# One FFN half-step with the activations as TensorE's stationary operand and 512 weight columns as its moving one

## The chip, the cores and the metric

The kernel runs on one core of a Trainium2 chip. TensorE (PE) multiplies a stationary 128x128 operand, which a weight load (PEld) brings in ahead, with a moving operand of up to 512 columns, into accumulators (PSUM, 8 banks of 128x512 float32 words). VectorE (DVE), ScalarE (ACT) and GpSimd (POOL) work on tiles in the on-chip memory; SyncE (SP) and ACT start DMAs. The metric is the time of one execution on the device in microseconds (us), the median of the runs.

## The reference

One encoder layer on a float32 residual x of 256 tokens by 2048 channels. Two FFN half-steps stand around a mixing block; the FFN's inner width is 5632:

```python
def swiglu(h, w_gate, w_up, w_down):
    return (jax.nn.silu(h @ w_gate) * (h @ w_up)) @ w_down
...
        h = rms_norm(x, ffn1_norm[l])
        x = x + FFN_RES_SCALE * swiglu(h, ffn1_w_gate[l], ffn1_w_up[l], ffn1_w_down[l])
...
        x = x + merged @ w_out
...
        h = rms_norm(x, ffn2_norm[l])
        x = x + FFN_RES_SCALE * swiglu(h, ffn2_w_gate[l], ffn2_w_up[l], ffn2_w_down[l])
    return rms_norm(x, final_norm)
```

## The kernel before, in words

Every float32 operand is split into a high part (a cast to float32r) and a low part (the rest), and a product is taken as high x high + high x low + low x high, three passes at one column a cycle.

**Layout.** x lies with channels on the partitions (`x[P, 16, 256]`). A norm's gained operand is `m`: for each of the 16 channel tiles k, 256 columns of high and 256 of low part. The norm's scale R (one number a token) is applied after the product.

**The stream.** All weights come as chunks of 1 MB (16 tiles of 128x128) in the order of their use: gate and up of the first FFN (`gu1`, 88 chunks), down (`dn1`, 44), the mixing block's, then `gu2`, `dn2`. SP loads chunks into three buffers (`raw`). `prep_upto` splits half a chunk at a time, a piece of 8 tiles: ACT casts the high part (`whi`, L125), DVE subtracts (`wlo`, L126), two pieces ahead of the product in the program.

**The products before.** In `run_stream` the weights are stationary. For each of a piece's 8 tiles one matmul with the high part streams 512 columns of `m`, high and low (L146); then one with the low part streams the 256 high columns (L151). So a piece is 8 matmuls of 512 columns and 8 of 256. A pair of output tiles (128 gate and 128 up columns) takes 32 weight tiles; its sums are in one PSUM tile `ps` of two banks, of which four are rotated. At its end `done` adds the two halves, multiplies by R, and writes silu(gate) * up as `G`, split into high and low: the moving operand of the down product, with FFN columns on the partitions, as the down product needs them. All 44 of an FFN's `G` tiles stay on the chip until the down product has used them.

**Order.** The engines run their own instructions in order; a scheduling layer sets that order and the semaphores from the program's order and the tiles that instructions touch. A wait on a PSUM tile is for the whole tile, both its banks.

**Down.** For each pair of output tiles 88 weight tiles against `G`; `residual` adds half the result to x, and the next norm's `m` follows.

Of the kernel before, what the change touches and what calls it, by code (L numbers as in the profile page):

```python
# [7 lines left out]
F32 = mybir.dt.float32  # L8
# [18 lines left out]
# the pairs of output tiles whose products are taken in turn, and the tiles of the contraction in each turn  # L27
GROUPS1 = [(3, 4)] + [(1, 8)] * 41
GROUPS2 = [(1, 8)] * 44

# columns of the packed per-channel parameters
# [11 lines left out]
def encoder_kernel(ctx: ExitStack, tc, xT, par, tab, gu1, dn1, win, gates_w, proj, wout, gu2, dn2, eye, outT):  # L43
# [8 lines left out]
    psum = ctx.enter_context(tc.tile_pool(name="psum", bufs=4, space=bass.MemoryType.PSUM))  # L52

# [5 lines left out]
    # an activation without data ahead of the first loads, so that the function table is there  # L59
# [14 lines left out]
    # the tensor engine's clock is up when the first weights come  # L74
# [5 lines left out]
    streams = [("gu1", gu1), ("dn1", dn1), ("win", win), ("gates", gates_w), ("proj", proj), ("wout", wout),  # L80
               ("gu2", gu2), ("dn2", dn2)]
    chunks, first_piece = [], {}
    for nm, ap in streams:
        first_piece[nm] = len(chunks) * (CH // PC)
        chunks += [ap[c] for c in range(ap.shape[0])]
    NPIECE = len(chunks) * (CH // PC)
# [28 lines left out]

    def prep_upto(q):
        while st["prep"] <= min(q, NPIECE - 1):
            i = st["prep"]
            c, h = divmod(i, CH // PC)
            load_upto(c + 2)  # L120
            src = raws[c][:, h * PC * P:(h + 1) * PC * P]
            hi = wspl.tile([P, PC * P], F32R, tag="whi", name="whi")
            lo = wspl.tile([P, PC * P], F32R, tag="wlo", name="wlo")
            for a, b in ((0, 4 * P), (4 * P, 8 * P)) if i == 0 else ((0, 8 * P),):
                ACT.copy(hi[:, a:b], src[:, a:b])  # L125
                DVE.tensor_tensor(lo[:, a:b], src[:, a:b], hi[:, a:b].bitcast(F32), ALU.subtract)  # L126
            pieces[i] = (hi, lo)
            if h == CH // PC - 1:
                del raws[c]
            st["prep"] += 1  # L130
# [3 lines left out]
    def run_stream(nm, ops, tile0=0, hooks={}):  # L134
        """ops: per weight tile (psum AP [P,512], moving AP [P,512], first, last, done)"""
        base = first_piece[nm] + tile0 // PC
# [19 lines left out]
    class Pair:  # L156
        """A pair of output tiles in two banks; taken when its first product is issued."""
# [62 lines left out]
    def gain_split(j, cg, mt):  # L220
        """x * gain of channel tiles 2j, 2j+1 as the moving operand"""
# [12 lines left out]
    def rms_scale(acc):  # L234
        """1 / sqrt(mean of squares + eps) of every token, on all partitions"""
# [21 lines left out]
    def ffn(gu_nm, dn_nm, m, R_get, after, groups, hooks={}, last=None, dn_hooks={}):  # L257
        G = []
        ops = []

        def gate_up(f):
            def done(ps):
                R = R_get()
                t = gather(ps)
                times_r(t, t, R)
                sl = work.tile([P, T], F32, tag="sl", name="sl")
                ACT.activation(sl, t[:, 0, :], AF.Silu)  # L267
                g = work.tile([P, T], F32, tag="g", name="g")
                DVE.tensor_tensor(g, sl, t[:, 1, :], ALU.mult)  # L269
                if f % 2 == 0:  # L270
                    G.append(unit_tile(F32R, name="G"))
                split_to(g, G[f // 2][:, f % 2, 0:256], G[f // 2][:, f % 2, 256:512])

            movs = [(lambda a, b, k=k: m[k // 2][:, k % 2, a:b]) for k in range(KD)]
            return movs, movs, done

        f = 0
        for n, cut in groups:
            ops += pair_ops([gate_up(f + i) for i in range(n)], cut)
            f += n  # L280
        run_stream(gu_nm, ops, 0, hooks)
        ops = []
        movs = [mov(G[k // 2], k % 2) for k in range(KF)]
        for j in range(KD // 2):
            def done(ps, j=j):
                residual(ps, j, 0.5)
                after(j)

            def last_done(ps, i):
                k = KD - 2 + i  # L290
# [446 lines left out]
```

## Time and profile before

| | us |
|---|---|
| median of 3 runs | 2018.48 (2018.42 to 2019.15) |
| span of the profiled execution, first to last instruction | 2016.2 |
| the runs' median over that span | 2.3 |
| TensorE busy | 2001.9 (99%) |
| DVE busy | 1258.1 (62%) |
| ACT busy | 1015.3 (50%) |
| first FFN's gate and up, down | 6.9 to 502.2, 502.2 to 748.0 |
| second FFN's gate and up, down | 1262.9 to 1755.4, 1755.4 to 2002 |

The profile is one execution; times in it are from the span's start. The profiled execution is known by its span alone, so a forecast is made as a difference to the span and put on the median. A matmul's record lasts longer than the distance to the next one's start, as they are pipelined; the distance is called its pace here, and the pace is what a stream of matmuls costs.

### The profile page before, as it was taken

To read this page: it belongs to the slowest core of one execution; us is meant where nothing else is said; L and a number is where in the kernel's file an instruction comes from. 1 tells how busy PE (TensorE), PEld (TensorE's weight loads), DVE (VectorE), ACT (ScalarE), POOL (GpSimd) and SP (SyncE) were. 2 spreads that over 40 slices of the span, in tenths; PEclk is the share of its full clock that TensorE was granted. 3 is DMA by queue.
4 is the path that set the end of the run, shared out by engine and by line. 5 is a ranking of instruction groups with operands and counts; after the bars stand their busy time and mean duration, and the time that the engine had idled before them with its cause. 6 is when DMAs were issued, how large, how long until landed. Compare 5 with 4: busy or idle time off the path is not lost.

```text
span 2016.2 us, 28231 instructions
## 1 busy us (share of the span) xinstructions
PE 2001.9 (99%) x11600; PEld 1767.7 (88%) x11600; DVE 1258.1 (62%) x1483; ACT 1015.3 (50%) x1332; POOL 0.2 (0%) x4
## 2 busy tenths in 40 slices
PE   9999999999999999999999999999999999999997
PEld 8888888888888888888888888888888888888887
DVE  8666666666554556765896766666666666645544
ACT  7444444444444445558865555544444444444442
POOL 0000000000000000000000000000000000000000
PEclk9999999999999999999999999999999999999998
DMA  7555555555555555545555555555555555555552
GB/s 274 188 188 189 188 188 188 188 188 188 188 188 188 188 188 199 188 147 188 188 188 188 188 189 190 186 188 188 188 189 187 190 188 188 188 190 188 189 188 101
DMA packets 54817, 377.90 MB, mean 187 GB/s; under 512 B 6304, under 2 KB 6944, under 8 KB 10016
## 3 DMA queue, kind: packets, MB, share of 16 engines
q1 hardware_dynamic: 54000, 375.51, 53.5%
q8 instruction: 90, 1.47, 0.3%
q10 hardware_dynamic: 688, 0.59, 0.1%
q14 instruction: 39, 0.32, 0.0%
HBM read 373.98 MB, written 2.10 MB: 187 GB/s over the span
## 4 chain that ended last, share of the span: by engine, by line
PE 99%; DVE 0%; DMA 0%; ACT 0%; SPq 0%; issue 0%; DVEq 0%
PE ps L146 63%; PE ps L151 33%; PE ps L148 1%; PE ps L149 1%; PE ps L439 0%; DMA raw<-gu 0%; DVE x L651 0%; PE ps L238 0%; PE ps L452 0%; PE ps L461 0%; PE ps L616 0%; PE ps L648 0%; PE ps L454 0%; ACT whi L125 0%; DVEq L732 0%
## 5 line engine op out<-in xcount | busy, mean ns | idle before, releaser
L126 DVE TENSOR_TENSOR wlo<-raw,whi 128x1024 fp32r<-128x1024 f32 (+1 forms) x709 | 866.4, 1223 | 679.1 <-ACT whi L125 678.1
L125 ACT CAST whi<-raw 128x1024 fp32r<-128x1024 f32 (+1 forms) x709 | 741.2, 1047 | 833.0 <-PE ps L146 577.6
L146 PE MATMUL ps<-m,whi 128*128 128x512 f32 x3712 | 932.5, 393 | 2.1 <-ACT whi L125 1.4
L146 PEld LDWEIGHTS ps<-m,whi 128*128 128x128 f32 x3712 | 668.0, 189 | 122.1 <-ACT whi L125 1.5
L151 PEld LDWEIGHTS ps<-m,wlo 128*128 128x128 f32 x3712 | 507.0, 191 | 36.0
L151 PE MATMUL ps<-m,wlo 128*128 128x256 f32 x3712 | 518.7, 282 | 0.0
L146 PE MATMUL ps<-G,whi 128*128 128x512 f32 x1320 | 330.5, 392 | 0.0
L146 PEld LDWEIGHTS ps<-G,whi 128*128 128x128 f32 x1320 | 237.4, 189 | 42.4
L151 PEld LDWEIGHTS ps<-G,wlo 128*128 128x128 f32 x1408 | 191.4, 190 | 12.9
L151 PE MATMUL ps<-G,wlo 128*128 128x256 f32 x1408 | 196.4, 282 | 0.0
L210 DVE TENSOR_TENSOR t<-ps,s 128x512 f32<-128x512 f32 x132 | 90.2, 683 | 0.3 <-ACT s L208 0.2
L217 ACT CAST G<-g 128x256 fp32r<-128x256 f32 x88 | 35.7, 407 | 108.5 <-DVE g L269 108.5
L214 DVE TENSOR_TENSOR t<-t,R 128x512 f32<-128x512 f32 x112 | 77.3, 691 | 3.5
L208 ACT COPY s<-ps 128x512 f32<-128x512 f32 x132 | 76.6, 580 | 0.2 <-ACT whi L125 0.2
L146 PE MATMUL ps<-mg,whi 128*128 128x512 f32 x256 | 64.1, 392 | 0.0
L218 DVE TENSOR_TENSOR G<-g,G 128x256 fp32r<-128x256 f32 x88 | 37.4, 426 | 39.2 <-ACT G L217 39.2
L146 PEld LDWEIGHTS ps<-mg,whi 128*128 128x128 f32 x256 | 46.0, 189 | 8.2
L151 PEld LDWEIGHTS ps<-mg,wlo 128*128 128x128 f32 x256 | 34.9, 190 | 2.5
L269 DVE TENSOR_TENSOR g<-sl,t 128x256 f32<-128x256 f32 x88 | 36.8, 419 | 0.5 <-ACT sl L267 0.5
L267 ACT ACTIVATE sl<-t 128x256 f32<-128x256 f32 x88 | 36.4, 415 | 0.6 <-DVE t L214 0.2
L151 PE MATMUL ps<-mg,wlo 128*128 128x256 f32 x256 | 35.7, 282 | 0.0
L146 PE MATMUL ps<-ya,whi 128*128 128x512 f32 x128 | 32.0, 392 | 0.0
(144 smaller groups left out, 672.0 us busy)
## 6 DMA issues: line engine op xcount, KB each, us to landing
raw<-gu SPq DMA_DIRECT2D x171, 1024.0 KB, 4.9
raw<-dn SPq DMA_DIRECT2D x88, 1024.0 KB, 4.8
raw<-gates_w SPq DMA_DIRECT2D x34, 1024.0 KB, 4.9
raw<-win SPq DMA_DIRECT2D x24, 1024.0 KB, 4.9
raw<-proj SPq DMA_DIRECT2D x16, 1024.0 KB, 4.9
raw<-wout SPq DMA_DIRECT2D x16, 1024.0 KB, 4.8
raw<-gu SPq DMA_DIRECT2D x9, 512.0 KB, 7.5
outT<-x SPq DMA_DIRECT2D x8, 256.0 KB, 2.4
```

The costliest lines, as they stand in the source:

```text
L125: ACT.copy(hi[:, a:b], src[:, a:b])
L126: DVE.tensor_tensor(lo[:, a:b], src[:, a:b], hi[:, a:b].bitcast(F32), ALU.subtract)
L146: nc.tensor.matmul(o[:, 0:512], lhsT=w, rhs=mv(0, 512), start=first, stop=False)
L148: nc.tensor.matmul(o[:, 0:256], lhsT=w, rhs=mv(0, 256), start=first, stop=False)
L151: nc.tensor.matmul(o[:, 0:256], lhsT=lo[:, t * P:(t + 1) * P], rhs=mv(0, 256), start=False, stop=last)
L208: ACT.copy(s, ps[:, :, 256:512])
L210: DVE.tensor_tensor(t, ps[:, :, 0:256], s, ALU.add)
L214: DVE.tensor_tensor(out, t, R.unsqueeze(1).to_broadcast([P, 2, T]), ALU.mult)
L217: ACT.copy(hi, src)
L218: DVE.tensor_tensor(lo, src, hi.bitcast(F32), ALU.subtract)
L267: ACT.activation(sl, t[:, 0, :], AF.Silu)
L269: DVE.tensor_tensor(g, sl, t[:, 1, :], ALU.mult)
```

## The change

In both FFNs the gate and up products turn round. A 128x128 tile of `m` (16 channel tiles, two halves of the tokens, high and low) is stationary and 512 weight columns move. The 5632 columns of gate and of up go in 11 blocks of 512; a chunk is now two channel tiles (a pair p) of a block's gate and up columns. A block has four accumulators, each a bank: P2 and P4 (gate, first and second 128 tokens), P3 and X (up). Every pair gives 8 products (`EIGHT`) of three matmuls of 512 columns, so 24 a chunk and 192 a block. P2 and P3 share one `ps` tile, P4 and X another. The list `SEVEN` and what belongs to it are not reached, since `SPLIT` is zero throughout.

Tokens are now on the partitions, so R is a column (`cols`) that goes into the silu's scale, and the result has to be turned: when the next block is at its fourth chunk, `turn` transposes 8 tiles of 128x128 on TensorE, ACT copies them out of PSUM and sends them to DRAM (`gd`, 512 KB a block). The down product loads a block (`gf`) two steps ahead and splits it into `G`; its first two pairs of output tiles are taken together, 4 contraction tiles at a time (`GROUPS_DN`), so that a new block is wanted every second piece. The weights' split tiles now come from the common pool `unit` (38 buffers in place of 30 and 8).

```diff
-    wspl = ctx.enter_context(tc.tile_pool(name="wspl", bufs=4))
-    unit = ctx.enter_context(tc.tile_pool(name="unit", bufs=30))
+    unit = ctx.enter_context(tc.tile_pool(name="unit", bufs=38))
...
+    def prep_eight(r, first):
+        out = {}
+        for i, names in ((0, ("B12", "B11")), (2, ("B21", "B22"))):
+            hi, lo = hi_lo(r[:, i:i + 2, :], ((1, 2), (0, 1)) if first and i == 0 else ((0, 2),))
...
+    EIGHT = [("P2", "A11", "B11"), ("P2", "A12", "B21"), ("P3", "A11", "B12"), ("P3", "A12", "B22"),
+             ("P4", "A21", "B11"), ("P4", "A22", "B21"), ("X", "A21", "B12"), ("X", "A22", "B22")]
...
+        pb = [new_ps() for _ in range(4)]
+        bank = {n: pb[i // 2][:, i % 2, :] for i, n in enumerate(("P2", "P3", "P4", "X", "P1", "P5", "P6", "P7"))}
...
+        def evict(b):
...
+                ACT.activation(a[:, 0, :], bank["P2"], AF.Silu, scale=R[:, 0:1])
+                ACT.copy(d[:, 0, :], bank["P3"])
+                ACT.activation(a[:, 1, :], bank["P4"], AF.Silu, scale=R[:, 1:2])
+                ACT.copy(d[:, 1, :], bank["X"])
+                def rest():
+                    for i in range(2):
+                        DVE.scalar_tensor_tensor(g[:, i, :], d[:, i, :], R[:, i:i + 1], a[:, i, :], ALU.mult, ALU.mult)
+                    return g
...
+        def turn(b, g):
+            o = pb[3]
+            for j in range(4):
+                for h in range(2):
+                    nc.tensor.transpose(o[:, j // 2, 256 * (j % 2) + P * h:256 * (j % 2) + P * (h + 1)],
+                                        g[:, h, P * j:P * (j + 1)], ident)
+            gt = unit_tile(F32, name="gt")
+            ACT.copy(gt, o)
+            nc.scalar.dma_start(gd[b], gt)
...
+                prep_upto(q + LOOK)
+                hooks.get(8 * b + n, lambda: None)()
+                if 8 * b + n == cols_at:
+                    norm.columns(pb[2])
+                if b and n == 0:
+                    late.append((b - 1, late.pop()()))
+                if b and n == 3:
+                    turn(*late.pop())
+                parts = pieces.pop(q)
+                for o, p, x, y in w:
+                    (xh, xl), (yh, yl) = act_part(norm, p, x), parts[y]
+                    for k, (l, r) in enumerate(((xh, yh), (xh, yl), (xl, yh))):
+                        nc.tensor.matmul(bank[o], lhsT=l, rhs=r, start=o not in begun, stop=left[o] == 0 and k == 2)
...
+            late.append(evict(b))
...
+        def ahead(t):
+            def run():
+                if t == 0:
+                    load_g(0)
+                    load_g(1)
+                    split_g(0)
+                    combine()
+                if t == 1:
+                    turn()
+                load_g(t + 2)
+                split_g(t + 1)
...
+        dn_hooks = dict(dn_hooks) | {2 * t: ahead(t) for t in range(NB)}
```

**TensorE inside a block.** The rows are of block 10 of the first FFN, at the end of its third chunk; `gb` is the product silu * up of block 9. Before, at a place in the stream with the same work (`m` against a piece's weights):

```order
L151 MATMUL ps_4391<-m_103,wlo_4354 128x256
L151 MATMUL ps_4391<-m_118,wlo_4354 128x256 x2
L151 MATMUL ps_4391<-m_155,wlo_4354 128x256 x2
L151 MATMUL ps_4391<-m_186,wlo_4354 128x256 x2
L146 MATMUL ps_4391<-m_212,whi_4387 128x512 [waits Activation_49]
```

and of the change:

```order
L416 MATMUL ps_149<-wlo_3173,m_165 128x512
L416 MATMUL ps_149<-whi_3172,m_165 128x512
L383 MATMUL ps_151<-ident_79,gb_3161 128x128 [waits DVE_49] x2
L383 MATMUL ps_151<-ident_79,gb_3161 128x128 x6
L416 MATMUL ps_148<-whi_3204,m_170 128x512 [waits Activation_49]
L416 MATMUL ps_148<-wlo_3205,m_170 128x512 [waits DVE_49]
```

All matmuls of the product have 512 columns now, and eight transposes stand between two chunks.

**TensorE from the last gate and up product to the first of down.** Before:

```order
L151 MATMUL ps_4391<-m_264,wlo_4409 128x256 x2
L151 MATMUL ps_4391<-m_291,wlo_4409 128x256 x2
L146 MATMUL ps_4487<-G_419,whi_4430 128x512 [waits Activation_49]
L146 MATMUL ps_4487<-G_419,whi_4430 128x512
L146 MATMUL ps_4487<-G_484,whi_4430 128x512 x2
```

and of the change (`gb_3443` is the last block's):

```order
L416 MATMUL ps_149<-wlo_3356,m_292 128x512
L416 MATMUL ps_149<-whi_3355,m_292 128x512
L383 MATMUL ps_151<-ident_79,gb_3443 128x128 [waits DVE_49]
L208 MATMUL ps_3474<-G_3458,whi_3385 128x512 [waits DVE_49,PE_49]
L208 MATMUL ps_3474<-G_3458,whi_3385 128x512
L208 MATMUL ps_3474<-G_3461,whi_3385 128x512 [waits DVE_49]
```

The first down product waited for its weights' cast alone; now it waits for DVE's split of `G`.

**ACT at the same place.** The rows of the change, in which L347 to L350 empty the last block's four accumulators and L279 casts the first `G` tiles:

```order
L144 CAST whi_3413<-raw_3315 128x1024
L347 ACTIVATE ga_3441<-ps_148,cols0_426 128x512 [waits PE_49]
L348 COPY gd_3442<-ps_148 128x512
L144 CAST whi_3450<-raw_3349 128x1024 [waits DMAHW1_49]
L349 ACTIVATE ga_3441<-ps_149,cols0_426 128x512 [waits PE_49]
L350 COPY gd_3442<-ps_149 128x512
L279 CAST G_3458<-gf_3454 128x2x256 [waits DMAHW4_49]
L279 CAST G_3461<-gf_3454 128x2x256
```

Before, ACT had only a copy of `ps` and small steps of the last pair here; now the cast of the first `G` stands behind the copy of the last accumulator. At the 18 inner blocks of both FFNs from the second on two casts of weights stand between L348 and L349 in place of one, and no cast of `G` follows.

## Rows read from the trace of the kernel before

**Rows 1.** Page, parts 1 and 2: busy time, and the granted clock in tenths.

```profile
PE 2001.9 (99%) x11600; PEld 1767.7 (88%) x11600; DVE 1258.1 (62%) x1483; ACT 1015.3 (50%) x1332; POOL 0.2 (0%) x4
PEclk9999999999999999999999999999999999999998
```

**Rows 2.** Page, part 4: the chain that ended last, by line.

```profile
PE ps L146 63%; PE ps L151 33%; PE ps L148 1%; PE ps L149 1%; PE ps L439 0%; DMA raw<-gu 0%; DVE x L651 0%; PE ps L238 0%; PE ps L452 0%; PE ps L461 0%; PE ps L616 0%; PE ps L648 0%; PE ps L454 0%; ACT whi L125 0%; DVEq L732 0%
```

**Rows 3.** Page, part 5: two costliest groups of PE (busy, mean ns | idle before).

```profile
L146 PE MATMUL ps<-m,whi 128*128 128x512 f32 x3712 | 932.5, 393 | 2.1 <-ACT whi L125 1.4
L151 PE MATMUL ps<-m,wlo 128*128 128x256 f32 x3712 | 518.7, 282 | 0.0
```

**Rows 4.** Timeline of PE at two places: start, duration, what, xcount.

```profile
502.20 2.00 PE L146 MATMUL ps<-G,whi 128*128 128x512 f32 x8
...
599.97 2.00 PE L146 MATMUL ps<-G,whi 128*128 128x512 f32 x8
601.81 1.12 PE L151 MATMUL ps<-G,wlo 128*128 128x256 f32 x8
602.76 0.63 PE L146 MATMUL ps<-G,whi 128*128 128x512 f32 x2
```

**Rows 5.** Timeline of PE, the last three of a run of eight.

```profile
531.29 0.84 PE L146 MATMUL ps<-G,whi 128*128 128x512 f32 x3
531.97 0.28 PE L151 MATMUL ps<-G,wlo 128*128 128x256 f32 x1
```

**Rows 6.** Timeline of PE near the end: one-column float32 products, then equal stationaries.

```profile
1996.38 0.95 PE L616 MATMUL ps<-ones,acc 128*128 128x1 f32 x8
1997.19 0.36 PE L148 MATMUL ps<-G,whi 128*128 128x256 f32 x1
...
1998.58 0.28 PE L149 MATMUL ps<-G,whi 128*128 128x256 f32 x1
1998.70 0.28 PE L148 MATMUL ps<-G,whi 128*128 128x256 f32 x1
1998.82 0.28 PE L149 MATMUL ps<-G,whi 128*128 128x256 f32 x1
```

**Rows 7.** ACT's groups by shape, 100 to 2000 us (busy, mean ns | idle before).

```profile
L125 ACT CAST whi<-raw 128x1024 fp32r<-128x1024 f32 x673 | 704.5, 1048 | 805.2 <-PE ps L146 561.6 <-issue 226.2 <-PE ps L149 11.7
L208 ACT COPY s<-ps 128x512 f32<-128x512 f32 x125 | 72.5, 580 | 0.2 <-ACT whi L125 0.2
...
L303 ACT ACTIVATE s<-ps 128x512 f32<-128x512 f32 x23 | 13.7, 596 | 0.0
...
L217 ACT CAST zt<-t 128x512 fp32r<-128x512 f32 x4 | 2.5, 619 | 0.4 <-DVE t L214 0.4
```

**Rows 8.** DVE's groups by shape.

```profile
L218 DVE TENSOR_TENSOR zt<-t,zt 128x512 fp32r<-128x512 f32 x4 | 2.7, 684 | 0.0
```

**Rows 9.** Timeline of the start.

```profile
6.93 0.73 PE L146 MATMUL ps<-m,whi 128*128 128x512 f32 x2 [1.35 <-ACT whi L125]
...
8.11 0.60 ACT L125 CAST whi<-raw 128x512 fp32r<-128x512 f32 x1
...
15.29 1.09 PE L146 MATMUL ps<-m,whi 128*128 128x512 f32 x4
```

**Rows 10.** Stretches of the start: busy by engine, PE's clock, DMA share, GB/s.

```profile
7.00:9.00 2.00, 1.28 (x4) 0.63 (x5) 1.74 (x4) 2.00 (x5) 0.00 (x0) 0.93 1.06 402
9.00:11.00 2.00, 2.00 (x5) 1.60 (x6) 1.80 (x3) 1.75 (x3) 0.00 (x0) 0.50 1.01 379
11.00:13.00 2.00, 2.00 (x12) 1.82 (x11) 1.88 (x3) 1.56 (x2) 0.00 (x0) 0.71 1.05 410
```

**Rows 11.** The first gate and up stretch, same columns (PE, PEld, DVE, ACT, POOL).

```profile
12.50:502.00 489.50, 489.50 (x2805) 430.75 (x2804) 318.01 (x400) 243.18 (x329) 0.00 (x0) 1.00 0.56 195
```

**Rows 12.** Timeline of PE at the first norm's sum of squares.

```profile
34.85 1.02 PE L238 MATMUL ps<-acc,ones 128*128 128x256 f32 x4
35.52 2.20 PE L146 MATMUL ps<-m,whi 128*128 128x512 f32 x8
```

More of the change, by code (lines that the diff above doesn't have):

```diff
@@ L25, with pair_order @@
 HT = 130
-GROUPS1 = [(3, 4)] + [(1, 8)] * 41
-GROUPS2 = [(1, 8)] * 44
+NB = F // 512
+SPLIT = [0] * 11
+GROUPS_DN = [(2, 4)] + [(1, KF)] * (KD // 2 - 2)
+def pair_order(s):
+    lead = 3 if s else 8
+    rest, seven = list(range(s, 8)), list(range(s))
+    out = rest[:lead]
+    rest = rest[lead:]
+    while rest or seven:
+        if seven:
+            out.append(seven.pop(0))
+        if rest:
+            out.append(rest.pop(0))
+    return out
 C_G1, C_GM, C_G2, C_GF = 0, 16, 32, 48
@@ new lines, in prep_seven, with put @@
+    def prep_seven(r):
+        out = {}
+        def put(names, parts):
+            for k, n in enumerate(names):
+                out[n] = (parts[0][:, k, :], parts[1][:, k, :])
+        t13 = unit_tile(F32, name="t13")
+        DVE.tensor_tensor(t13, r[:, 0:4:3, :], r[:, 1::-1, :], ALU.subtract)
+        put(("B11", "B21"), hi_lo(r[:, 1:3, :]))
+        t24 = unit_tile(F32, name="t24")
+        DVE.tensor_tensor(t24[:, 0, :], r[:, 3, :], t13[:, 0, :], ALU.subtract)
+        DVE.tensor_tensor(t24[:, 1, :], r[:, 2, :], t24[:, 0, :], ALU.subtract)
+        b22 = unit_tile(F32R, name="b22")
+        ACT.copy(b22[:, 0, :], r[:, 3, :])
+        DVE.tensor_tensor(b22[:, 1, :], r[:, 3, :], b22[:, 0, :].bitcast(F32), ALU.subtract)
+        out["B22"] = (b22[:, 0, :], b22[:, 1, :])
+        put(("T2", "T4"), hi_lo(t24))
+        put(("T1", "T3"), hi_lo(t13))
+        return out
@@ L116, in prep_upto @@
     def prep_upto(q):
-        while st["prep"] <= min(q, NPIECE - 1):
+        while st["prep"] <= min(q, len(items) - 1):
             i = st["prep"]
-            c, h = divmod(i, CH // PC)
+            c, kind = items[i]
             load_upto(c + 2)
[L121 to L128, printed above, removed]
+            r = raws[c].rearrange("p (s w) -> p s w", s=4)
+            if kind == "seven":
+                pieces[i] = prep_seven(r)
+            elif kind == "eight":
+                pieces[i] = prep_eight(r, i == 0)
+            else:
+                hi, lo = hi_lo(r[:, 2 * kind:2 * kind + 2, :])
+                pieces[i] = tuple(z.rearrange("p a w -> p (a w)") for z in (hi, lo))
+            st["prep"] += 1
+            if st["prep"] == len(items) or items[st["prep"]][0] != c:
@@ new lines, in encoder_kernel, with act_part @@
+    SEVEN = [("P2", "A12", "B21"), ("P3", "S4", "B22"), ("P4", "A22", "T4"), ("P1", "A11", "B11"),
+             ("P5", "S1", "T1"), ("P6", "S2", "T2"), ("P7", "S3", "T3")]
+    def act_part(norm, p, name):
+        i = int(name[1:])
+        if name[0] == "S":
+            t = norm.sm[p]
+            return tuple(t[:, z, P * (i - 1):P * i] for z in range(2))
+        row, k = i // 10 - 1, i % 10 - 1
+        t = norm.m[p]
+        return tuple(t[:, k, 256 * z + P * row:256 * z + P * (row + 1)] for z in range(2))
@@ new lines, in ffn, with load_g, split_g @@
+    def ffn(gu_nm, dn_nm, norm, after, cols_at, hooks={}, last=None, dn_hooks={}):
+        gd = [dram.tile([P, 2, 512], F32, name=f"{dn_nm}_{b}") for b in range(NB)]
+        combine, turn = gate_up(gu_nm, norm, hooks, gd, cols_at)
+        G, raw_g = [], []
+        def load_g(b):
+            if b < NB:
+                t = unit_tile(F32, name="gf")
+                nc.sync.dma_start(t, gd[b])
+                raw_g.append(t)
+        def split_g(b):
+            if b < NB:
+                for i in range(2):
+                    G.append(unit_tile(F32R, name="G"))
+                    split_to(raw_g[b][:, i, :].rearrange("p (a t) -> p a t", a=2), G[-1][:, :, 0:256], G[-1][:, :, 256:512])
+        def ahead(t):
[9 more added lines that the diff above has]
+                split_g(t + 1)
+            return run
+        dn_hooks = dict(dn_hooks) | {2 * t: ahead(t) for t in range(NB)}
+        movs = [(lambda a, b, k=k: G[k // 2][:, k % 2, a:b]) for k in range(KF)]
+        jobs = []
@@ L295, in ffn @@
             else:
[L296 removed]
+                ops += pair_ops(jobs[j:j + n], cut)
+            j += n
         run_stream(dn_nm, ops, 0, dn_hooks)
@@ L321, in square, with sums, columns @@
             sq_acc(j, self.acc)
+        def sums(self, p):
+            xg = work.tile([P, 2, T], F32, tag="t", name="xg", bufs=3)
+            for i in range(2):
+                ACT.activation(xg[:, i, :], x[:, 2 * p + i, :], AF.Copy, scale=col(self.cg + 2 * p + i))
+            sf = work.tile([P, 4, P], F32, tag="s", name="sf")
+            a11, a21, a12, a22 = (xg[:, k, P * h:P * (h + 1)] for k in range(2) for h in range(2))
+            DVE.tensor_tensor(sf[:, 0, :], a21, a22, ALU.add)
+            DVE.tensor_tensor(sf[:, 2, :], a11, a21, ALU.subtract)
+            DVE.tensor_tensor(sf[:, 1, :], sf[:, 0, :], a11, ALU.subtract)
+            DVE.tensor_tensor(sf[:, 3, :], a12, sf[:, 1, :], ALU.subtract)
+            t = unit_tile(F32R, name="sm")
+            split_to(sf.rearrange("p a t -> p (a t)"), t[:, 0, :], t[:, 1, :])
+            self.sm[p] = t
+        def columns(self, tot):
+            for h in range(2):
+                for i in range(2):
+                    nc.tensor.matmul(tot[:, h, 0:1], lhsT=self.acc[:, i, h * P:(h + 1) * P], rhs=ones[:, 0:1],
+                                     start=i == 0, stop=i == 1)
+            self.cols = const.tile([P, 2], F32, name=f"cols{self.cg}")
+            root_columns(tot, self.cols)
         def tile_ready(self, j):
```

168 lines of the change are left out of this document (110 added, 58 removed).

## The prediction

> **What bounds the kernel now.** I read the page's busy times first: TensorE is busy 2001.9 of 2016.2 us at the full clock [rows 1]. The chain that ended last says the same, 96% of it in the two matmul lines of the stream [rows 2], and the page's groups show how little that stream waits: 2.1 us before the high matmuls, nothing before the low ones [rows 3]. So the time is the number of matmuls times their pace, plus whatever makes TensorE wait. DVE and ACT have room: in the first gate and up stretch they work 318.0 and 243.2 of 489.5 us, and the DMA share is 0.56 [rows 11]. The reader should therefore not ask what becomes cheaper on ACT or DVE, but how many columns TensorE streams, at which pace, and where it stands still.
>
> **The columns.** They stay the same. Before, an FFN's gate and up take 88 chunks x 16 tiles x (512 + 256) columns = 1,081,344; after, 11 blocks x 192 x 512 = 1,081,344. What changes is that 2816 matmuls of two lengths become 2112 of one, so only what a matmul costs beside its columns can be won.
>
> **The pace before.** A piece of 8 + 8 matmuls starts at 502.20, and one 35 pieces later at 599.97 [rows 4]: 97.77 / 35 = 2.793 us a piece. 176 pieces are 491.6 us an FFN, 983.2 for both.
>
> **The pace after.** In such a piece the eight 512-column matmuls take 1.84 us and the eight short ones 0.95 [rows 4], 0.230 and 0.119 each. The run is not even: its last three take 0.68 us from 531.29 to 531.97 [rows 5], 0.227 each, so the first ones, behind the short ones, are slower. From 0.227 and 0.119 a column costs (0.227 - 0.119) / 256 = 0.42 ns, 1 / 2.4 GHz, and about 0.013 us a matmul lies beside the columns. A stream with 512 columns throughout has no short ones ahead, so I take 0.227: 2 x 2112 x 0.227 = 958.8 us, **24.4 less**. Upper bound: the mean of a run, 0.230, gives 971.5 and 11.7 less. Lower bound: of three matmuls the second has the first one's stationary, and if that saved the 0.013, it would be 1408 x 0.013 = 18.3 more. Against it: L148 and L149 use one stationary twice, and their starts are 0.12 apart whether it is new or not [rows 6].
>
> **The transposes.** 11 x 8 x 2 = 176, of float32 with a 128x128 stationary and 128 moving columns; nothing else runs on TensorE meanwhile. No such operation is in the trace. Low: one record of 128 columns, 128 x 0.42 ns + 0.013 = 0.067 each, 11.8 us in all. High: float32 matmuls stand in the trace as two records (L616's four as x8); that way 2 x 0.101 each, 35.6 us. The nearest row is that of L616, a full float32 stationary with one moving column, hence the load's price: 8 records take 1996.38 to 1997.19, 0.81 us [rows 6]. Eight transposes of one record each with such loads are 0.81 us a block: **+17.8**. That the input is float32 and a load of 128 columns outlasts 54 ns of moving columns puts it nearer to this row than to the low end.
>
> The Trainium skill ("TensorE: Matmul & The Clock Gate", Part 4: PE-mode transpose) gives about 275 ns for a transpose in a kernel, so 176 would cost an estimated 48 us; rows here show records of 0.25 to 0.4 us at paces of 0.10 to 0.23, so I read that figure as a record's length, which a stream doesn't pay.
>
> **From gate and up to down, twice.** Before, the stream runs through here: the first product of down (502.20) needs `G` tiles made long ago, and the last `G` is wanted some 40 tiles later. After, the cast of the first `G` stands on ACT behind the four reads of the last block's accumulators. Counted from E, when TensorE could start its next matmul: the last product's record outlasts its pace by 0.393 - 0.227 = 0.17 us [rows 3, 5]; then the silu on P4 (it waits for the tile that X ends) as L303, 0.60, the copy of X as L208, 0.58, the cast of a `G` tile, 0.62 [rows 7], DVE's rest, 0.68 [rows 8]; with some 0.1 for four hand-overs, E + 2.75. Two matmuls later the second `G` tile's rest is 0.2 late. Sum 3.0 us, **+6.0** for both. Late next would be the blocks behind; they are wanted every 5.6 us and cost ACT 1.2 and DVE 1.4 us each, beside ACT's 2.1 for the weights, so they keep ahead. Low bound: without the silu's wait 2.3 each, 4.6. High bound: TensorE's clock. At the start, where TensorE paused between its first matmuls, the granted clock was 0.93, 0.50 and 0.71 in three stretches of 2 us (the lower of its levels is 1.2 GHz), a loss of 0.14 + 1.0 + 0.58 = 1.7 us [rows 10]. If each stop of 3 us did that, +3.4.
>
> **The start.** The first matmul needs the second part of the first weights; its cast was done at 8.11 + 0.60 = 8.71 [rows 9], against 6.93 for the first matmul before. 24 matmuls from there, 5.45 us, and 1.7 for the clock end at 15.9. Before, two pieces (5.59 us of work) were done at 15.29. So **+0.7**; bounds 0 and 1.8, the whole shift.
>
> **Edits at nothing.** (a) The norm's sum: eight one-column records, 0.81 [rows 6], for four of L238, 0.67 [rows 12]: +0.3 for both, counted. (b) Reading the accumulators, per block 2.4 us on ACT, the copy of the transposes some 1.2 (twice L208), DVE's products 1.4: behind 43.6 us of matmuls, in which the weights take 16.8 of ACT. What they cost if late is a rival below. (c) The DMAs: gate and up write 0.5 MB per 43.6 us; in down's first 62 us, 1.5 MB instead of 1 MB per 5.6 us, 281 GB/s. The start shows 379 to 410 GB/s [rows 10], so these loads stay hidden behind the look-ahead of three chunks; without it ACT would stand at `gf`, about 1 us a block. SP starts them between the weights' loads, in line, ACT the stores with `gt` ready, so nothing waits in those queues. (d) The common pool: same 38 buffers, and ACT waits for TensorE's release of them as it did (561.6 us before L125 [rows 7]). (e) The old gathers go from ACT and DVE, which TensorE didn't wait for.
>
> **Sum.** -24.4 + 17.8 + 6.0 + 0.7 + 0.3 = +0.4 on a span of 2016.2; on the median of 2018.48 that is **2018.9**. About 0.2% (4 us) is what a measurement of this kernel can tell from no change; the forecast is no change, a small gain in pace spent on turning the result. With all small terms at their own bounds it runs from -5.6 (transposes at 11.8) to about +5.
>
> **Rivals.**
> 1. *Faster: the price beside the columns shrinks.* If a repeated stationary spares its 0.013, 18.3 us go: 2000.6; with cheap transposes alone 2012.9, with both 1994.6. For it: the run's pace falls from its first to its last matmul, and the trace has no longer run. Against: rows 6. Chance 0.30 for more than 4 us, of which I put most at the cheap transposes.
> 2. *Slower: a transpose is two records.* Then +17.8: 2036.7. For it: all float32 matmuls of the trace. Against: a transpose only moves data. 0.12. With a stop between transposes, each paying a one-column record's 0.25 us, 176 x 0.25 = 44, which is 2045: 0.04.
> 3. *Slower: the accumulators are read too late.* There is no second set: a block's first product on P4, 12 x 0.227 = 2.72 us behind its start, waits for the copy of X. ACT reads P2 and P3 from -2.55 to -1.37 (P3's last product ends 12 matmuls before the block's end), makes two casts until +0.73, then the silu and the copy until +1.91. The slack is 0.8 us; it decides when ACT's two reads with two casts come later than that, by a cast that waits for its weights or a slower silu. Half a us late at 18 blocks and little elsewhere: +9, 2028. For it: two casts on ACT before the reads; against: ACT is idle half the time. 0.12. The Trainium skill ("Perfetto Trace Analysis", Optimizing Tensor Performance, Matmuls) advises to rotate groups through different banks so that their reading overlaps the next group, which this change gives up; the rows leave it the 0.8 us.
> 4. *Slower: the pace stays at the run's mean*, 0.230: 12.7 more, 2031.6. Against: the last three of a run are steady. 0.09.
>
> The forecast, within 4 us, has 0.33. So faster 0.30, same 0.33, slower 0.37. The range goes from 2004 to 2037: it takes in the cheap transposes, the slower cases 2 to 4 at their prices, and leaves out a saving on every repeated stationary and transposes with stops, with what lies beyond the prices about 0.2.
>
> **What would show it.** L416's starts 0.227 apart in the middle of a block, and a block's 192 in 43.6 us; 176 transpose records with 0.81 us for eight, in one group between two chunks; TensorE idle before the first down matmul by 2.5 to 3 us twice, released by DVE's `G`; no idle at a block's 13th matmul; gate and up of an FFN in about 490 us. Wrong would be: 352 transpose records, a pace off by 0.003, idle time before L416 released by ACT's `gd`, or a clock that falls behind the stops.

## The result, and the profile after

The changed kernel takes 2041.32 us (median of 4 runs, 2038.72 to 2043.14) against 2018.45 for the kernel before on the same chip: a ratio of 1.0113, with a 95% interval of 1.0099 to 1.0127. That is 22.9 us more, where no change was forecast, and it lies above the range of 2004 to 2037. The span of its profiled execution is 2040.0 us.

The page's busy times, and the shares of the chain that ended last by engine and by line:

```profile
PE 2004.3 (98%) x10376; PEld 1717.1 (84%) x10376; DVE 1103.8 (54%) x1217; ACT 965.8 (47%) x1221; POOL 0.2 (0%) x4
...
PE 93%; DVE 4%; ACT 2%; issue 1%; DMA 0%; SPq 0%; DVEq 0%; ACTq 0%
PE ps L416 47%; PE ps L208 28%; PE ps L213 15%; PE ps L383 1%; PE ps L210 1%; PE ps L211 1%; DVE wlo L145 1%; ACT whi L144 1%; DVE v L606 1%; DVE t L272 0%; ACT s L270 0%; DMA raw<-gu 0%; DVE x L855 0%; DVE uu L726 0%; DMA tbt<-tab 0%
```

Compared with [rows 1, 2], TensorE's busy time grew by only 2.4 us, but the chain now goes 7% of its way through other engines: through the casts of the weights' high parts and the subtractions of their low parts (L144, L145) and through steps of the mixing block (L606, L272). That is a sign of stops in TensorE. Where they are is shown by cutting the span into its stages. A row gives the stretch and its length, then busy time and count of PE, PEld, DVE, ACT and POOL, PE's clock, DMA share and GB/s. Before, for the mixing block up to its `proj` product and for the second gate and up:

```profile
748.01:1084.11 336.10, 336.10 (x1999) 298.45 (x1998) 239.96 (x294) 218.61 (x313) 0.00 (x0) 1.00 0.53 183
...
1262.88:1755.37 492.49, 492.49 (x2822) 433.37 (x2821) 309.74 (x359) 237.09 (x313) 0.00 (x0) 1.00 0.54 188
```

After, the first gate and up, the first down, the mixing block up to `proj`, and the second gate and up:

```profile
9.07:502.45 493.38, 491.12 (x2201) 406.67 (x2202) 236.37 (x255) 220.91 (x261) 0.00 (x0) 1.00 0.57 211
502.45:752.36 249.91, 248.54 (x1415) 218.44 (x1416) 135.12 (x143) 110.45 (x136) 0.00 (x0) 0.99 0.56 204
752.36:1108.00 355.64, 341.49 (x1998) 300.89 (x1997) 242.51 (x296) 214.28 (x312) 0.00 (x0) 0.99 0.47 171
1286.88:1778.26 491.38, 489.12 (x2203) 405.55 (x2202) 221.97 (x209) 209.45 (x239) 0.00 (x0) 1.00 0.55 205
```

| us | before | after | change |
|---|---|---|---|
| start to the first down product | 502.20 | 502.45 | +0.3 |
| first down | 245.81 | 249.91 | +4.1 |
| mixing block up to `proj` | 336.10 | 355.64 | **+19.5** |
| `proj` and `wout` | 178.77 | 178.88 | +0.1 |
| second gate and up | 492.49 | 491.38 | -1.1 |
| second down and end | 260.83 | 261.74 | +0.9 |

The rebuilt product costs about what was forecast. Most of the loss lies in the mixing block, whose products, loops and tiles the change does not touch. TensorE does the same matmuls there (x1998 for x1999), and was busy throughout before, while now it stands for 14 us and works some of the rest at a lower clock. The list of its waits in the whole kernel says for what (total, times, longest), and a row of the first down product shows the one of these eight that is not in the mixing block:

```profile
PE ps L208 <- ACT whi L144: 10.8, 6, 2.9
PE ps L213 <- DVE wlo L145: 3.7, 2, 2.0
...
573.47 2.14 PE L208 MATMUL ps<-G,whi 128*128 128x512 f32 x8 [1.37 <-ACT whi L144]
```

TensorE waits for the weights' split, which before it did for 1.4 us in the whole kernel [rows 3]. ACT is not short of time: it is busy 60% of the stage. What is wrong is when it comes to the casts. ACT's timeline after, in the mixing block (idle time and its releaser in brackets):

```profile
789.09 0.59 ACT L270 COPY s<-ps 128x512 f32<-128x512 f32 x1 [4.68 <-PE ps L213]
791.16 0.62 ACT L279 CAST zt<-t 128x512 fp32r<-128x512 f32 x1 [1.49 <-DVE t L276]
791.69 3.89 ACT L144 CAST whi<-raw 128x1024 fp32r<-128x1024 f32 x4
...
806.27 0.62 ACT L279 CAST tch<-tbc 128x512 fp32r<-128x512 f32 x1 [3.32 <-DMA tbc<-tab]
...
807.60 3.88 ACT L144 CAST whi<-raw 128x1024 fp32r<-128x1024 f32 x4
```

and before, at a like place in the same stage:

```profile
770.53 1.05 ACT L125 CAST whi<-raw 128x1024 fp32r<-128x1024 f32 x1 [1.75 <-PE ps L146]
771.48 0.61 ACT L217 CAST zt<-t 128x512 fp32r<-128x512 f32 x1
772.00 0.58 ACT L208 COPY s<-ps 128x512 f32<-128x512 f32 x1
773.31 1.05 ACT L125 CAST whi<-raw 128x1024 fp32r<-128x1024 f32 x1 [0.73 <-ACT s L208]
```

Before, one cast follows another at TensorE's pace of 2.8 us a piece, most of them released by TensorE giving a buffer back, and `s` and `zt` stand between two casts with hardly a wait of their own (none in these rows, 0.44 us before the next `zt`). After, ACT first stands 4.68 us for the end of a pair (`s`), then 1.5 for DVE, casts `zt`, and only then makes the four casts of the next pair in one go. In the whole stage the waiting for TensorE has passed from the casts to `s`; before and after:

```profile
ACT whi L125 <- PE ps L146: 84.7, 63, 1.8
```

```profile
ACT s L270 <- PE ps L213: 81.2, 24, 7.9
```

At 789 two pieces, 5.6 us of work, lie ready for TensorE and cover all this: it is busy in 19.75 of the 19.80 us from 786 to 805.8. Behind the next pair the loads of two tables (3.32 us) come on top, and the two pieces no longer suffice. TensorE's timeline at that place:

```profile
804.64 1.11 PE L213 MATMUL ps<-m,wlo 128*128 128x256 f32 x8
808.69 3.78 PE L208 MATMUL ps<-m,whi 128*128 128x512 f32 x8 [2.94 <-ACT whi L144]
812.27 1.91 PE L213 MATMUL ps<-m,wlo 128*128 128x256 f32 x8
813.98 2.25 PE L208 MATMUL ps<-m,whi 128*128 128x512 f32 x8
```

It stands 2.94 us, and then eight matmuls take 3.78 us that take 2.00 at the full clock [rows 4]. The stretches of that time show the clock (same columns as the stages):

```profile
802.00:809.00 7.00, 4.06 (x26) 3.52 (x25) 2.69 (x6) 3.26 (x6) 0.00 (x0) 0.91 0.28 79
809.00:815.00 6.00, 6.00 (x20) 5.04 (x20) 4.30 (x4) 2.48 (x3) 0.00 (x0) 0.54 0.49 164
```

The clock lacks 0.09 x 7 + 0.46 x 6 = 3.4 us of full speed, a part of it while TensorE still stands. By the starts the piece from 808.69 to 813.98 takes 5.29 us for 2.79 and the next eight matmuls 0.25 more: 2.75 us, so this stop costs nearly twice its length.

### The profile page after: what moved, and what is told of

Read it like the earlier page. It is cut to its first block, busy times and chain, and to the rows that moved or that the text cites. A ratio compares the mean times of both kernels' runs of the same rounds, so it can differ in the third digit from the quotient of the medians.

```text
span 2040.0 us, 25119 instructions
## 1 busy us (share of the span) xinstructions
PE 2004.3 (98%) x10376; PEld 1717.1 (84%) x10376; DVE 1103.8 (54%) x1217; ACT 965.8 (47%) x1221; POOL 0.2 (0%) x4
## 4 chain that ended last, share of the span: by engine, by line
PE 93%; DVE 4%; ACT 2%; issue 1%; DMA 0%; SPq 0%; DVEq 0%; ACTq 0%
PE ps L416 47%; PE ps L208 28%; PE ps L213 15%; PE ps L383 1%; PE ps L210 1%; PE ps L211 1%; DVE wlo L145 1%; ACT whi L144 1%; DVE v L606 1%; DVE t L272 0%; ACT s L270 0%; DMA raw<-gu 0%; DVE x L855 0%; DVE uu L726 0%; DMA tbt<-tab 0%
## 5 line engine op out<-in xcount | busy, mean ns | idle before, releaser
L145 DVE TENSOR_TENSOR wlo<-raw,whi 128x1024 fp32r<-128x1024 f32 (+1 forms) x709 | 830.4, 1219 | 662.0 <-ACT whi L144 658.6
L416 PE MATMUL ps<-whi,m 128*128 128x512 f32 x2816 | 874.6, 390 | 3.4 <-ACT whi L144 3.4
L144 ACT CAST whi<-raw 128x1024 fp32r<-128x1024 f32 (+1 forms) x709 | 702.2, 1050 | 222.5 <-DMA raw<-gu 91.5
L416 PEld LDWEIGHTS ps<-whi,m 128*128 128x128 f32 x2816 | 529.2, 188 | 113.1 <-ACT whi L144 3.7
L416 PE MATMUL ps<-wlo,m 128*128 128x512 f32 x1408 | 548.4, 389 | 0.0
L416 PEld LDWEIGHTS ps<-wlo,m 128*128 128x128 f32 x1408 | 264.8, 188 | 54.7 <-DVE wlo L145 0.3
L208 PE MATMUL ps<-m,whi 128*128 128x512 f32 x896 | 228.2, 396 | 10.0 <-ACT whi L144 9.4
L208 PEld LDWEIGHTS ps<-m,whi 128*128 128x128 f32 x896 | 162.1, 190 | 40.4 <-ACT whi L144 10.8
L347 ACT ACTIVATE ga<-ps,cols 128x512 f32<-128x512 f32 x22 | 15.2, 690 | 289.5 <-PE ps L416 289.5
L213 PEld LDWEIGHTS ps<-m,wlo 128*128 128x128 f32 x896 | 122.9, 192 | 13.0 <-DVE wlo L145 4.6
L213 PE MATMUL ps<-m,wlo 128*128 128x256 f32 x896 | 126.6, 284 | 3.7 <-DVE wlo L145 3.7
L272 DVE TENSOR_TENSOR t<-ps,s 128x512 f32<-128x512 f32 x44 | 30.3, 689 | 72.9 <-ACT s L270 72.9
L270 ACT COPY s<-ps 128x512 f32<-128x512 f32 x44 | 25.7, 583 | 90.0 <-PE ps L213 90.0
L476 ACT ACTIVATE s<-ps 128x512 f32<-128x512 f32 x23 | 13.7, 597 | 109.7 <-PE ps L213 109.7
```

The source lines that it names most:

```text
L144: ACT.copy(hi[:, a:b, :], src[:, a:b, :])
L145: DVE.tensor_tensor(lo[:, a:b, :], src[:, a:b, :], hi[:, a:b, :].bitcast(F32), ALU.subtract)
L208: nc.tensor.matmul(o[:, 0:512], lhsT=w, rhs=mv(0, 512), start=first, stop=False)
L213: nc.tensor.matmul(o[:, 0:256], lhsT=lo[:, t * P:(t + 1) * P], rhs=mv(0, 256), start=False, stop=last)
L416: nc.tensor.matmul(bank[o], lhsT=l, rhs=r, start=o not in begun, stop=left[o] == 0 and k == 2)
```

## The experiments

**Theory.** The weights' tiles and the stage's own (`zt`, `vh`, `v`, the tables, `m`) now come out of one pool, `unit`. A pool gives its buffers out in the program's order, so a cast of weights can no longer stand on ACT ahead of a tile of `unit` that the program names before it. The lead of the casts shrinks to the two pieces of look-ahead that the program writes, less whatever the tile ahead of them waits for. **Rivals:** the 38 buffers are too few for all comers; or the new traffic through DRAM delays loads.

### e1: a pool of their own for the weights outside gate and up

```diff
-    unit = ctx.enter_context(tc.tile_pool(name="unit", bufs=38))
+    wspl = ctx.enter_context(tc.tile_pool(name="wspl", bufs=4))
+    unit = ctx.enter_context(tc.tile_pool(name="unit", bufs=30))
...
-                hi, lo = hi_lo(r[:, 2 * kind:2 * kind + 2, :])
+                hi, lo = hi_lo(r[:, 2 * kind:2 * kind + 2, :], own=True)
```

> The changed kernel, with the pool wspl of four buffers a tag back for the pieces of the streams outside gate and up, and 30 buffers in unit; the two FFN blocks stay as changed. Theory (the common pool): with one pool the casts of the weights stand on ACT in program order behind the stage's own tiles, so a late s, zt or table stops TensorE; with a pool of their own they run ahead as before. The mixing stage up to the projection goes from 355.6 back to about 336.1 us and the stop of 1.65 us at 571.8 goes too: 2041.3 - 19.5 - 1.6 = 2020, between 2018 and 2023, and TensorE's 10.8 us of waits in front of L208's matmuls that L144's cast ends shrink to under 2. Rival A (the new traffic of the turned results through DRAM delays the later loads): no change, 2041. Rival B (38 buffers in one pool serve better than 30 and 4 apart): slower than 2041.

Measured: 2018.87 us (10 runs), a ratio to before of 1.0005 (0.9996 to 1.0014). The mixing block up to `proj`, and TensorE's waits of more than 2 us in the whole kernel:

```profile
750.51:1086.60 336.09, 336.09 (x1998) 298.45 (x1997) 239.69 (x294) 218.57 (x313) 0.00 (x0) 1.00 0.54 184
```

```profile
PE ps L211 <- DVE G L283: 5.0, 2, 2.5
PE ps L419 <- ACT whi L147: 2.4, 1, 2.4
```

The stage is back at 336.1 with TensorE busy in all of it, and the stop at 571.8 in the first down product (the row at 573.47 above) has gone too. ACT's casts wait for TensorE's release again, 82.9 us in this stage. What waits are left are the two boundaries to down, and the start. The number of bytes of buffers is the same as in the changed kernel (30 + 8 for 38), and so is the traffic, so neither rival explains the 22.5 us between them. (A pool apart also keeps eight buffers for the weights alone; e8 tells that from the order.)

### e2: the kernel before with the common pool

```diff
-    wspl = ctx.enter_context(tc.tile_pool(name="wspl", bufs=4))
-    unit = ctx.enter_context(tc.tile_pool(name="unit", bufs=30))
+    unit = ctx.enter_context(tc.tile_pool(name="unit", bufs=38))
...
-            hi = wspl.tile([P, PC * P], F32R, tag="whi", name="whi")
-            lo = wspl.tile([P, PC * P], F32R, tag="wlo", name="wlo")
+            hi, lo = (unit_tile(F32R, name=n).rearrange("p a w -> p (a w)") for n in ("whi", "wlo"))
```

> The kernel before, with one edit: the two tiles of a weight piece come out of unit, with 38 buffers, instead of a pool of their own. Gate and up, gathers and all else as before. Theory (the common pool): the mixing stage alone pays, 748.01 to 1084.11 grows from 336.1 us by 15 to 20, and the kernel takes 2034 to 2040. Rival A (the loss comes with the turned results and their traffic, which this kernel does not have): 2018.5, the mixing stage 336 us.

Measured: 2046.44 us, 1.014 (1.0124 to 1.0155). The common pool alone, without any of the new product, loses 28 us, more than expected. The first gate and up and the mixing block:

```profile
7.07:509.00 501.93, 497.74 (x2820) 436.91 (x2821) 317.21 (x407) 243.73 (x336) 0.00 (x0) 0.99 0.52 193
754.82:1109.40 354.58, 340.71 (x1998) 300.13 (x1997) 242.66 (x296) 214.21 (x312) 0.00 (x0) 1.00 0.47 172
```

The mixing block pays 18.5 us, as expected. The old gate and up pays as well, 6.7 and 4.7 us, which the expectation left out: TensorE stops once in each, 3.47 us before 48 and 2.88 before 1309, for casts that stand on ACT behind the `sl` and `G` of the first pairs, and the clock is at half behind the first of them (0.50 from 48 to 52). So the effect is the pool's, not the new product's.

### e3: three pieces of look-ahead in the common pool

```diff
-            prep_upto(q + LOOK)
+            prep_upto(q + 3)
```

(in `run_stream` only.)

> The changed kernel with three pieces of look-ahead instead of two in the streams outside gate and up; the common pool of 38 stays. Theory (order on ACT): each cast gets one piece more of slack, 2.8 us, where the stops in the mixing stage are 0.6 to 3.2 us long, so most of them go: 2041.3 less 14 to 19 is 2022 to 2027. Rival B (the casts wait for buffers that are still held, not for their turn on ACT): a third piece takes four more half-used tiles out of the same 38, so nothing is won, 2041 or more. Rival A (traffic): 2041.

Measured: 2027.61 us, 1.0047 (1.0032 to 1.0062). 13.7 of the 22.9 us come back from one piece more of lead, a little less than expected, with the same 38 buffers; a shortage of buffers would have got worse. The mixing block takes 341.8 us, and the largest stop left in it is one of 2.2 us, at 1043.

### e6 and e7: fewer buffers, in the common pool and in a pool apart

```diff
-    unit = ctx.enter_context(tc.tile_pool(name="unit", bufs=38))
+    unit = ctx.enter_context(tc.tile_pool(name="unit", bufs=34))
```

> The changed kernel with 34 instead of 38 buffers in the common pool. Theory (order on ACT: the casts stand behind the stage's own tiles, and wait for those, not for buffers): the stops in the mixing stage stay as they are, 2041, within 4 us. Rival (the common pool is short of buffers, the casts wait until TensorE and DVE give some back): four buffers less, two pieces' worth, make every stop longer by up to a piece, 2.8 us each at ten or more stops: 2060 or more.

Measured: 2049.11 us, 1.0154 (1.0139 to 1.0169), between the two expectations. Seven stops from 569 to 868 stay as they were, 0.7 to 3.1 us from start to start, which speaks for the order. But one at 1001 has grown, and the clock falls behind it; there the changed kernel and e6:

```profile
1001.00:1014.00 13.00, 9.52 (x54) 7.89 (x53) 12.97 (x19) 8.22 (x13) 0.00 (x0) 1.00 0.24 83
```

```profile
1001.00:1014.00 13.00, 7.64 (x32) 6.41 (x31) 12.90 (x20) 9.50 (x14) 0.00 (x0) 0.74 0.25 86
```

22 matmuls fewer fit into these 13 us. What ACT stands for there, ahead of the cast that TensorE needs, in the changed kernel and in e6:

```profile
1003.79 0.91 ACT L631 ACTIVATE gt<-t,pr 128x256 f32<-128x256 f32 x2 [3.21 <-DVE t L276]
```

```profile
1004.21 1.28 ACT L631 ACT_TABLE_LOAD   x1 [6.84 <-DVE t L276]
```

In both it is a tile of the stage's own, `gt`, that waits for DVE while the cast stands behind it, but longer in e6. So the number of buffers matters in that part of the mixing block too; whether by the order that it leads to or by itself is not shown. The mixing block takes 7.4 us more than in the changed kernel (363.07 us for 355.64), half of it idle time of TensorE (17.75 us for 14.15), the rest longer busy time, at a lower clock in part (0.74 above).

e7 is e1 with three buffers a tag in `wspl` and 32 in `unit`:

> The kernel with the pool wspl (e1), but three buffers a tag in it and 32 in unit, the least that a look-ahead of two pieces can hold. Theory, narrow: what counts is that the pieces have a pool of their own, so that their casts need not keep their place behind s and zt: 2019 to 2022. Rival: what counts is the fourth buffer, a piece more of lead; with three the lead is two pieces, as in the changed kernel, and the stops of over 2 us come back in part: 2028 to 2038.

Measured: 2018.36 us, 1.0002 (0.9992 to 1.0011). Three buffers apart do what four do: the separation counts, not the fourth buffer.

### e8: the mirror, a pool of their own for `zt`

```diff
+    ztp = ctx.enter_context(tc.tile_pool(name="ztp", bufs=4))
+    unit = ctx.enter_context(tc.tile_pool(name="unit", bufs=34))
...
-            zt = unit_tile(F32R, name="zt")
+            zt = ztp.tile([P, 2, 512], F32R, tag="zt", name="zt")
```

> The mirror of e1: in the changed kernel the weights stay in unit, now with 34 buffers, and only the four zt tiles have a pool of their own, of four (38 buffers in all). Theory (a cast keeps its place behind every tile of unit that the program names before it): between the four zt, from about 752 to 800 us, the casts no longer come four in a row behind zt but one for each piece that TensorE ends, and the stop of 2.1 us at 770 goes; behind the tables (805), the v and vh tiles (822, 835) and from 1001 on, whose tiles are still in unit, the stops stay. The time: 2041.3 - 2.0 = 2039, or with the price of 34 buffers as in e6, 2049.1 - 2.0 = 2047. Rival (it is a special property of the weights' own ring, or the number of buffers): the stop at 770 and the bursts of four stay, 2041 to 2049.

Measured: 2039.22 us, 1.0105 (1.0089 to 1.0122). ACT's timeline, first among the `zt`, then behind them at the first `vh`, whose tile is still in `unit`:

```profile
772.20 2.00 ACT L145 CAST whi<-raw 128x1024 fp32r<-128x1024 f32 x2 [1.05 <-DMA raw<-win]
774.10 0.57 ACT L271 COPY s<-ps 128x512 f32<-128x512 f32 x1
775.38 0.62 ACT L280 CAST zt<-t 128x512 fp32r<-128x512 f32 x1 [0.70 <-DVE t L277]
775.91 1.99 ACT L145 CAST whi<-raw 128x1024 fp32r<-128x1024 f32 x2
...
812.93 0.62 ACT L280 CAST vh<-v 128x512 fp32r<-128x512 f32 x1 [2.28 <-DVE v L607]
813.46 3.89 ACT L145 CAST whi<-raw 128x1024 fp32r<-128x1024 f32 x4
```

Up to 790 casts go ahead of `s` and `zt`, mostly two at a time, as far as the loads let them; the stop at 770 is gone, and with the lead that they have won the one at the tables too, which I had expected to stay. At `vh` the burst of four and the stops behind it (1.58 us each) are as before the edit, and the long stop at 994 (5.35 us) is that of e6. That 2039 was met is luck: two stops (1.83 and 2.94 us) went, with the slow clock behind the second, where 2.0 us had been counted, and the price of 34 buffers was paid, which 2039 leaves out. The weights did not get a ring or a reserve of their own here; one group of tiles was taken out of their way. So up to 813 the order in the shared pool is the cause. For the stops behind that, e1, e3 and e7 show that it is the pool; which tile stands ahead of the casts is read from ACT's rows there, and not tested one by one.

### e4: the first `G` blocks earlier

e1, with one edit: the first two blocks are loaded, and the first one split, behind the fifth chunk of the last gate and up block.

```diff
+        def first_g():
+            load_g(0)
+            load_g(1)
+            split_g(0)
+        combine, turn = gate_up(gu_nm, norm, dict(hooks) | {8 * (NB - 1) + 5: first_g}, gd, cols_at)
...
-                    load_g(0)
-                    load_g(1)
-                    split_g(0)
```

> The kernel with the pool wspl of four buffers (e1), and the first two G blocks of down loaded, and the first one split, in the last block of gate and up behind its fifth chunk instead of at down's first step. Theory: the two stops of 2.74 us in front of down's first product go, and with them the fall of the granted clock behind the first one, 1.7 us: 7.2 us less than e1, so 2013 if e1 takes 2020. A rival: the gap before down moves but stays, because the second G block, which is stored from the last accumulators, or the last block's combine on ACT is late next: 2 to 3 us less only, 2017 to 2018. Another: the casts of G inside the block delay ACT's reads of the accumulators and the next block's first product: no gain.

Measured: 2012.7 us (10 runs), 0.9973 (0.9963 to 0.9983): faster than both kernels. TensorE at the boundary in e1, and in e4:

```profile
499.40 0.39 PE L419 MATMUL ps<-whi,m 128*128 128x512 f32 x1
499.63 0.27 PE L386 MATMUL ps<-ident,gb 128*128 128x128 f32 x1
502.38 2.05 PE L211 MATMUL ps<-G,whi 128*128 128x512 f32 x4 [2.48 <-DVE G L283]
```

```profile
499.65 0.39 PE L419 MATMUL ps<-whi,m 128*128 128x512 f32 x1
499.88 1.98 PE L211 MATMUL ps<-G,whi 128*128 128x512 f32 x8
```

The stop has gone whole, and so has the low clock behind it, which e1 shows (below: 502 to 504 and 504 to 508) and e4 does not (1.00 throughout):

```profile
502.00:504.00 2.00, 1.62 (x4) 1.37 (x5) 2.00 (x4) 1.07 (x3) 0.00 (x0) 0.54 0.00 0
504.00:508.00 4.00, 4.00 (x19) 3.37 (x19) 1.42 (x3) 1.05 (x1) 0.00 (x0) 0.80 0.00 0
```

0.46 x 2 + 0.20 x 4 = 1.7 us. With two stops of 2.75 that makes 7.2 expected; the runs give 6.2, the spans 6.7. The slow clock is not there in every execution: in the profiled one of e7, which has the same two stops, the clock behind the first is

```profile
502.72:508.00 5.28, 5.28 (x29) 4.59 (x30) 3.55 (x5) 2.10 (x4) 0.00 (x0) 1.00 0.00 0
```

and it is 1.00 behind the second as well.

### e5: e4 without the transposes

```diff
-                    nc.tensor.transpose(o[:, j // 2, 256 * (j % 2) + P * h:256 * (j % 2) + P * (h + 1)],
-                                        g[:, h, P * j:P * (j + 1)], ident)
...
-            ACT.copy(gt, o)
+            ACT.copy(gt, g)
```

> The kernel with the pool wspl and the early first G blocks (e4), without TensorE's transposes: the copy into gt reads the products g themselves, so the turning is left out and down gets blocks whose rows and columns are not turned; all else, with its DMAs, stays. Forecast's term: eight transposes take 0.81 us of TensorE's time, 22 blocks 17.8; by the records of the changed kernel 0.79 for seven steps and about 0.10 more, 22 x 0.89 = 19.6 at most. So 2012.7 - 17.5 = 2195 less 200, that is 1995, between 1993 and 1997. Rival: the transposes stand in a place where the next product waits anyway, for the four reads of the accumulators or for its weights: then less comes back, 2003 or more. Rival: a transpose also slows the products behind it (a change from float32 to the rounded format and back): more comes back, 1990 or less.

(The 2195 in it is a slip; 2012.7 - 17.5 is 1995.2.) Measured: 1993.52 us, 0.9877 (0.986 to 0.9893). The transposes cost 19.2 us, 0.87 a block. TensorE around eight of them in the changed kernel:

```profile
71.57 1.03 PE L383 MATMUL ps<-ident,gb 128*128 128x128 f32 x8
72.36 0.47 PE L416 MATMUL ps<-whi,m 128*128 128x512 f32 x1
72.67 0.39 PE L416 MATMUL ps<-wlo,m 128*128 128x512 f32 x1
```

From the first transpose to the next product it is 0.79 us, and that product's successor starts 0.31 behind it in place of 0.23: 0.87 together.

## Why the prediction was wrong

**The step that failed is (d): "The common pool: same 38 buffers, and ACT waits for TensorE's release of them as it did".** It was put down at nothing; undoing it in the streams outside gate and up gives back 2041.32 - 2018.87 = 22.5 us (e1), and putting the common pool alone into the kernel before costs 28 (e2). The number of buffers was the same, but their number was not what the pool of before was worth. The idle time of 561.6 us that TensorE's release ended [rows 7] was read as a wait that would stay. It was the evidence of a lead: with a ring of their own the casts ran on until no buffer was free, past whatever the stage's own tiles waited for. In the common pool they keep their place behind those tiles, and the two pieces left of the lead cover a pair's end (4.68 + 1.49 us of ACT's waiting, no stop at 789) but not a longer wait, such as the tables' 3.32 us on top. By the spans e1 gives back 21.6 us: 19.5 are the mixing block's (355.64 for 336.09), and 1.8 the first down product's (249.91 for 248.13), where `m` and its wait stand before the casts and TensorE stops at 571.8.

**The fall of the clock** was a bound, at nothing in the sum. It came behind the first boundary (1.7 us, the size taken from the start) and not behind the second, where TensorE stood as long; and behind the stop at 805 (2.75 by the starts). "A clock that falls behind the stops" was among the signs of being wrong.

The other steps held, by the runs:

- **The pace.** In e1's second gate and up 491.39 us, less ten groups of transposes at 0.87, the stop of 2.75 and 1.0 for the norm's sum (by so much the first of e5's blocks there is longer than the others, 44.50 us for 43.52), are 478.9 for 2112 matmuls: 0.227, as forecast. Neither a saving on a repeated stationary (rival 1) nor the run's mean of 0.230 (rival 4) came.
- **The transposes.** 176 records, one each, and no stop between them: rival 2 is out. The term of 17.8 was 1.4 too small. The row of one-column products was the right one to take: eight of them took 0.81 us and eight transposes with 128 columns 0.79, so the columns do not show in the price. What was left out is that the product behind a group has its successor late, 0.31 for 0.23. The trace of before has the same behind its one-column products, 0.20 from the start at 1997.19 [rows 6] to the next one at 1997.39 (first row below), where 0.12 is usual. The Trainium skill ("TensorE: Matmul & The Clock Gate", Part 4: PE-mode transpose) gives about 275 ns for a transpose in a kernel, beside a figure for a bfloat16 tile; the records here, of float32, last 0.27 us, which agrees, but in a group they start 0.1 us apart, so the estimate of 48 us from it was 2.5 times what e5 measured.
- **The accumulators** (rival 3) were read in time. In the changed kernel from 45 to 490 us TensorE is busy in all 445.0, and in both FFNs the 13th matmul of a block starts 0.23 us behind the 12th, so no block began late, though two casts stand between the reads. The advice of the Trainium skill ("Perfetto Trace Analysis", Optimizing Tensor Performance, Matmuls) to rotate groups through banks had nothing to win here.
- **The boundary.** The last product starts at 499.48 and the first of down at 502.45; with 0.23 for the product, 2.74 us stand between, for which 2.75 was worked out. The 0.2 for the second `G` came as well; it is seen at the second boundary, at the full clock, where the first eight matmuls take 2.00 us to the next start for 1.84 [rows 4] (last two rows below).
- **The start.** The first matmul came at 9.07, for 8.71 forecast, and at 8.10 in e1.

The rows of the kernel before, behind its one-column products, and of the changed kernel at the second boundary:

```profile
1997.39 0.28 PE L149 MATMUL ps<-G,whi 128*128 128x256 f32 x1
```

```profile
1778.26 2.16 PE L208 MATMUL ps<-G,whi 128*128 128x512 f32 x8 [0.86 <-DVE G L280]
1780.26 1.11 PE L213 MATMUL ps<-G,wlo 128*128 128x256 f32 x8
```

With (d) undone the forecast of 2018.9 meets the 2018.87 of e1, which is closer than its terms are. By the spans e1 is 2.2 us above the kernel before, where the sum said 0.4: gate and up, with their stops and transposes, came out 1.3 below the sum (502.38 for 502.20, and 491.39 for 492.49), the two down products 3.1 above it (248.13 for 245.81, 261.63 for 260.83). Of these 3.1, 1.7 is the clock, and the rest is about the price of the eleventh group of transposes of each FFN, which the sum counts with gate and up but which runs within down (seven of its eight records, at 509.53 in e1); in e7, without the slow clock, the first down takes 246.66. No rival covered (d): it was weighed as a count of buffers, and ACT's order was looked at in gate and up alone, not in the stages that the diff leaves as they are.

Left open: what of the long stop at 1001 in e6 (994 in e8) is the number of buffers and what a different order there. It was not taken apart, and no kernel with more than 38 buffers in the common pool was run.

## What to carry to other kernels

A pool is an order as well as a store. Where a stream of loads or casts runs ahead of its stage, moving its tiles into a pool that others share ties it to the slowest tile named before it, even with as many buffers; look for it in the stages that the change does not touch, in the order of the engine that prepares the operands. An idle time ended by the release of a buffer is the sign that an engine has a lead, so ask what keeps that lead after a change. And where an engine near full use must wait for the first operand of its next stage to be prepared, because another engine does something else first, prepare that operand one step earlier: here that was worth 6.2 us and made the new product faster than the old one (2012.7 against 2018.2).

## What was not expected of the hardware

Stops of the same length before the same products had different consequences. In the changed kernel 2.74 us at the first boundary brought the granted clock to 0.58 from 504 to 508, and the like at the second left it at 1.00. It is not the place: of the two profiled executions with stops of 2.75 there, that of e1 has the slow clock behind the first (0.54 from 502 to 504), that of e7 behind neither.

Nor is it the length alone. The stop of 2.94 us at 808 brought six us at about half, and those of 1.83 and 1.58 us before 772 and 824 none (1.00 from 771 to 776 and from 823 to 829). But in e6 the stop before the same products as at 772, of 1.78 us, brought 0.72 from 769 to 775, and in e3 one of 1.84 brought 0.57 from 1045 to 1049. So a stop of 1.8 us can bring the slow clock and one of 2.75 need not, and what decides is not shown by these runs.
